# A two-block mixer on one core: attention's value product with float32 probabilities, two key tiles at a time in the two halves of the array's columns

## The chip, the core and the metric

The kernel runs on one core of one Trainium2 chip. The metric is the device time of one execution in microseconds; the median of several runs counts. One execution is profiled, and its trace is what the rows further down come from.

## What is computed

The program is a first block of two layers, then a second block of three mixers and a mixture of experts. The change lies in the first block's attention alone. Each layer has 8 heads; queries and keys have 96 features, values 64. In the first layer the 1024 tokens of `x` attend to all 1280 tokens (256 of the context and 1024 of `x`), and the 256 context tokens to themselves; in the second layer only the tokens of `x` have queries.

```python
def attend(q, k, v):
    ...
    def one_block(qi):
        s = jnp.einsum('bqhd,bkhd->bhqk', qi, k).astype(jnp.float32) * sm_scale
        p = jax.nn.softmax(s, axis=-1).astype(v.dtype)
        return jnp.einsum('bhqk,bkhd->bqhd', p, v)
```

Everything is float32, so products need more than the tensor engine's single pass over rounded operands.

## The kernel before, in words

**Products.** The kernel's usual form of an exact product is `mm3` (L100): each operand is two parts of type float32r, a high part rounded as the tensor engine does and the remainder, and three products (high by high, high by low, low by high) are summed in one PSUM bank; they are recorded under L104, L105 and L106. A product whose operands are plain float32 is one call in the text too, and two passes, each a weight load and a MATMUL, in the trace.

**Attention** (`attention`, L742) treats heads in pairs. `prepare` (L800) makes queries, keys and values of a pair by tokens, `turn` (L867) puts features on partitions in two parts by transposes (L876), `maxima` (L881) finds every query's largest score by products into the two banks `s1` (L891) and reductions on VectorE (L892), and puts it as one more row beside the queries (L900). `attend` (L905) does the rest, with keys on partitions: for a chunk of up to 512 queries and each tile of 128 keys, scores (L922), the exponential on ScalarE (L926), the probabilities in two parts (`ph`, a copy on ScalarE at L930 or in each chunk's second tile on VectorE at L928; `pl`, a subtraction at L931, every third one on GpSimd), and, three tiles later (`LAG`), three products with the values into one bank:

```python
v1, vl = vv[:, jv, hd, 64:], vv[:, jv, hd, :64]
nc.tensor.matmul(po[:65, :n], v1, ph, start=jv == 0, stop=False)
nc.tensor.matmul(po[:64, :n], vl, ph, start=False, stop=False)
nc.tensor.matmul(po[:65, :n], v1, pl, start=False, stop=jv == nk - 1)
```

These are L937, L938 and L939. The values `vv` hold a low part, a high part (L835 and L836) and a column of ones, so that row 64 of the result is the sum of the probabilities. At the end of a chunk ScalarE copies the bank (L942), the sums are put on the queries' partitions by one-row transposes (L946), inverted (L948), spread along the queries again by products with the identity (L952), multiplied into the gate (L954) and, on GpSimd, into the result (L955), which GpSimd's queue writes to DRAM (L956).

**Order.** Chunks are 256, 512 and 512 queries in the first layer (2, 10 and 10 key tiles) and 512 and 512 in the second. The loop at L967 takes the heads one after another; after every step of `attend` it advances the generators of the next pair's `prepare` and the next head's `turn` and `maxima` by set rates (`RP`, `RM`). That is the order of the text. The instructions on an engine are then placed by the library when the program is built, by when it expects their operands to be ready, earlier ones in the text first; once built, each engine's order is fixed. PSUM's 8 banks are three for scores (`st`), two for maxima (`s1`), and one each for the value product (`po`), for turns and sums (`tr`) and for `prepare` (`pre`). `up` holds the probabilities in `UB` buffers.

Of the kernel before, what the change touches and what calls it, by code (L numbers as in the profile page):

```python
# [20 lines left out]
P = 128  # L21
D = 1024
# [17 lines left out]
class K:  # L40
    """Engines, pools and constants that all phases share."""
# [23 lines left out]
    def psum(self, **bufs):  # L65
        """Banks by what they are for."""
        if self._ps:
            self._ps.close()
        self._ps = ExitStack()
        self.bufs = bufs or dict(mm=5, tr=2, po=1)  # L70
        self.ps = self._ps.enter_context(self.tc.tile_pool(name="ps", bufs=1, space=PSUM, reuse_waits="tile"))
# [7 lines left out]
    def rsqrt(self, out, in_, scale, eps):  # L79
        """out = (in_ * scale + eps) ** -0.5"""  # L80
# [8 lines left out]
    def split(self, hi, lo, src, scale=None, eng=None):  # L89
        """hi + lo = src (* scale, one number per partition), hi rounded as the tensor engine does."""  # L90
# [9 lines left out]
    def mm3(self, out, a, b, start, stop):  # L100
        """out += a^T b with both operands in two parts."""
# [6 lines left out]
    def mm_packed(self, both, top, a2, ah, bh, bl, start, stop):  # L108
        """both += a2^T bh and top += ah^T bl; a2 has the two parts of a side by side, top is both's first half,
        and the sum of both's halves is a^T b."""  # L110
# [8 lines left out]
    def vectors(self, pool, name, rows):  # L119
        """Vectors from DRAM (each a multiple of P long) as columns [P, n]: {key: column range}."""  # L120
# [16 lines left out]
    def bcast_row(self, out, col):  # L137
        """out[:, j] = col[j] for every partition: a column of P numbers as a row on all partitions."""
# [5 lines left out]
def vec(ap):  # L144
    """A DRAM vector (n * P,) as rows [n, P]."""
    return ap.rearrange("(n p) -> n p", p=P)


def gemv(k, pool, out, cs, w, b, ncols, chunk=128, group=4, tag="mm", ttag="tr", bufs=4):
    """out[:, j, :] = w[:, j * P:(j + 1) * P]^T cs + b[:, j], cs [P, KD, 2]; in steps."""  # L150
# [22 lines left out]
def run(gen, n=None):  # L173
    """The next n steps of a generator, or all that are left."""
# [19 lines left out]
HID = 99  # L194
PLP = 3
LAG = 3
UB = 6
# [23 lines left out]
def beside(main, side, n):  # L221
    """Steps of main, with n of side after every one."""
# [16 lines left out]
def put_h(k, wp, xn, tok, hh, hl, g, sh, onv=2):  # L239
    """(xn * g + sh) for a token tile, transposed and in two parts; onv of four features' tiles on the vector  # L240
    engine."""
# [20 lines left out]
def load_w(k, pool, w, c0, n, kt=KD, scale=None, tag="w", wmax=P, ktmax=KD, bufs=2, rbufs=2, rpool=None):  # L262
    """Columns c0..c0+n of w [kt * P, :] in two parts, [P, kt, n]."""
# [12 lines left out]
def head_weights(k, pool, I, l, pr, v, own=None):  # L276
    """Weights of a pair of heads' queries, and of its keys and values, in two parts, scaled by the norms'; in the
    places of the input product's weights, the parts in the pool own if there is one."""
# [15 lines left out]
class Columns:  # L294
    """Weights' tiles of P columns one after another, in turns in two pools; the first may be loaded ahead."""
# [12 lines left out]
def product(k, w, h, t0, n):  # L308
    """A bank with w^T h over n tokens from t0 on."""
# [7 lines left out]
def silu_out(k, sg, ps, dst):  # L317
    """silu(ps) into DRAM by way of sg."""
# [16 lines left out]
def block1(k, I, x_open, x_out, ahead, fill):  # L335
    """The first block: both layers; x_open(pool), then x_out(pool, t, tile) for the x token tiles, and
    what x_open returns, each of which returns what is to be done later; ahead: the next
    block's first weights, then a product with them; fill(pool): steps to be done beside the second layer's attention."""
    nc, tc = k.nc, k.tc
    A = nc.vector  # L340
    with ExitStack() as es:
# [16 lines left out]
        def early(pool=None):  # L358
            """The second layer's first weights, then a product with them."""
# [7 lines left out]
        def vectors(l):  # L367
            """The layer's vectors and tables."""
# [21 lines left out]
        def modulation(l, gp, **kw):  # L390
            """Shift and scale, then the gate."""
# [11 lines left out]
        def second(gp, **kw):  # L403
            """What the second layer needs."""
# [13 lines left out]
        def begin(wp):  # L418
            """The first layer's input."""
# [25 lines left out]
        for l in range(2):  # L445
# [26 lines left out]
            def weights():  # L472
                """In the place of what only the preparations need: the output's weights."""
# [15 lines left out]
def in_proj(k, I, l, last, h, vecs, keep, wp, ydram, sga_d, begin):  # L489
    """The layer's input product and its two convolution branches; begin(pool) makes the input."""  # L490
# [5 lines left out]
    with ExitStack() as es:  # L496
# [6 lines left out]
        def each(c0, n, cks, fn):  # L503
            """fn(feature tile, chunk of tokens, PSUM) over columns c0..c0+n of the input's product."""
# [2405 lines left out]
```

## Time and profile before

| | us |
|---|---|
| median of 3 runs | 4433.74 |
| lowest and highest | 4425.26, 4436.02 |
| span of the profiled execution | 4414.7 |
| TensorE (PE) busy, 22375 products | 4045.3 |
| VectorE (DVE) busy | 2878.1 |
| ScalarE (ACT) busy | 1983.2 |
| GpSimd (POOL) busy | 1231.9 |

The span runs from the first to the last instruction of the profiled execution, whose whole time is not listed apart; it is set beside the median of the runs. PE stands for products, PEld for the weight loads that overlap them. A product's recorded time is longer than the distance to the next one, because products are pipelined: what it costs is read from the starts.

### The profile page before, as it was taken

To read this page: it belongs to the slowest core of one execution; us is meant where nothing else is said; L and a number is where in the kernel's file an instruction comes from. 1 tells how busy PE (TensorE), PEld (TensorE's weight loads), DVE (VectorE), ACT (ScalarE), POOL (GpSimd) and SP (SyncE) were. 2 spreads that over 40 slices of the span, in tenths; PEclk is the share of its full clock that TensorE was granted. 3 is DMA by queue.
4 is the path that set the end of the run, shared out by engine and by line. 5 is a ranking of instruction groups with operands and counts; after the bars stand their busy time and mean duration, and the time that the engine had idled before them with its cause. 6 is when DMAs were issued, how large, how long until landed. Compare 5 with 4: busy or idle time off the path is not lost. (4 is left out here: it accounts for less than half of the span.)

```text
span 4414.7 us, 61941 instructions
## 1 busy us (share of the span) xinstructions
PE 4045.3 (92%) x22375; PEld 3077.3 (70%) x22376; DVE 2878.1 (65%) x5659; ACT 1983.2 (45%) x4292; POOL 1231.9 (28%) x1211
## 2 busy tenths in 40 slices
PE   7999899999998999999997999999898898899993
PEld 5787666667776666788785788777776566666672
DVE  4684577764745778646764555667776676776775
ACT  4122366653112766423443133433256566666664
POOL 1201133332101333321334331122313333343233
PEclk9999999999999999999997999899999999999996
DMA  6121400123123001334434411215368888888885
GB/s 187 34 64 43 123 13 13 33 83 107 41 61 102 11 10 36 121 117 129 126 118 136 122 34 33 74 44 189 110 228 264 242 265 247 256 276 264 269 274 165
DMA packets 371316, 558.81 MB, mean 127 GB/s; under 512 B 52126, under 2 KB 285056, under 8 KB 346048
## 3 DMA queue, kind: packets, MB, share of 16 engines
q1 hardware_dynamic: 335728, 432.81, 30.5%
q0 software_dynamic: 35280, 122.02, 10.7%
q8 instruction: 177, 2.90, 0.3%
q14 instruction: 131, 1.07, 0.1%
HBM read 438.42 MB, written 116.33 MB: 126 GB/s over the span
## 5 line engine op out<-in xcount | busy, mean ns | idle before, releaser
L95 DVE TENSOR_TENSOR wa_lo<-w_raw,wa_hi 128x512 fp32r<-128x512 f32 x520 | 338.1, 685 | 18.6 <-ACT wa_hi L94 17.8
L94 ACT ACTIVATE wa_hi<-w_raw 128x512 fp32r<-128x512 f32 x520 | 299.7, 626 | 59.9 <-PE mm L106 24.9
L104 PE MATMUL mm<-hh,w_hi 128*128 128x512 f32 (+1 forms) x848 | 320.0, 377 | 4.7 <-ACT h L256 4.7
L105 PE MATMUL mm<-hl,w_hi 128*128 128x512 f32 (+1 forms) x848 | 318.7, 376 | 0.0
L106 PE MATMUL mm<-hh,w_lo 128*128 128x512 f32 (+1 forms) x848 | 317.1, 374 | 0.0
L104 PE MATMUL mm<-wa_hi,xh 128*128 128x512 f32 (+3 forms) x632 | 268.0, 424 | 2.8 <-ACT xh L94 2.7
L106 PE MATMUL mm<-wa_hi,xl 128*128 128x512 f32 (+3 forms) x632 | 259.4, 410 | 3.6 <-DVE xl L95 3.6
L105 PE MATMUL mm<-wa_lo,xh 128*128 128x512 f32 (+3 forms) x632 | 261.3, 414 | 1.2 <-DVE wa_lo L95 1.2
L892 DVE TENSOR_REDUCE mx<-mm 128x1 f32<-128x512 f32 (+1 forms) x400 | 225.1, 587 | 53.2 <-PE mm L891 50.7
L926 ACT ACTIVATE pe<-mm 128x512 f32<-128x512 f32 (+1 forms) x336 | 193.2, 588 | 144.3 <-PE mm L106 115.5
L931 POOL TENSOR_TENSOR pl<-pe,ph 128x512 fp32r<-128x512 f32 x96 | 142.0, 1482 | 335.4 <-ACT ph L930 326.5
L931 DVE TENSOR_TENSOR pl<-pe,ph 128x512 fp32r<-128x512 f32 (+1 forms) x240 | 204.6, 864 | 38.1 <-ACT ph L930 36.8
L2698 POOL COPY wc<-xg 128x1 f32<-128x1 f32 (+5 forms) x97 | 79.6, 820 | 508.4 <-DMA xg<-h_d,ix 502.3
L2635 POOL DMA_INDIRECT acc_d<-ye,ix x97 | 168.7, 1740 | 182.5 <-ACT hidh L94 73.4
L159 PE MATMUL mm<-gemv_w,b_c_cs 128*2 128x128 f32 x1536 | 199.0, 286 | 10.2 <-DMA gemv_w<-in_w_mod_dram 7.1
L2631 ACT ACTIVATE ye<-mm,wc 128x512 f32<-128x512 f32 (+5 forms) x194 | 127.6, 680 | 176.7 <-DMA acc_d<-ye,ix 125.1
L595 DVE SCALAR_TENSOR_TENSOR acc<-zc,b_v,acc 128x512 f32<-128x512 f32 (+1 forms) x300 | 199.3, 713 | 1.5
L104 PEld LDWEIGHTS mm<-hh,w_hi 128*128 128x128 f32 x848 | 161.3, 190 | 40.1 <-issue 7.6
L105 PEld LDWEIGHTS mm<-hl,w_hi 128*128 128x128 f32 x848 | 161.4, 190 | 33.8 <-issue 7.0
L94 ACT ACTIVATE w_hi<-w_raw 128x1024 fp32r<-128x1024 f32 x61 | 64.6, 1059 | 262.5 <-PE mm L105 227.2
L106 PEld LDWEIGHTS mm<-hh,w_lo 128*128 128x128 f32 x848 | 161.2, 190 | 28.1 <-issue 0.4
L930 ACT ACTIVATE ph<-pe 128x512 fp32r<-128x512 f32 (+1 forms) x296 | 178.0, 625 | 4.1
(779 smaller groups left out, 11572.8 us busy)
## 6 DMA issues: line engine op xcount, KB each, us to landing
w_raw<-in_exp_w_dram SPq DMA_DIRECT2D x192, 1024.0 KB
w_raw<-in_w_in_dram SPq DMA_DIRECT2D x69, 512.0 KB
gemv_w<-in_w_mod_dram SPq DMA_DIRECT2D x48, 512.0 KB
gemv_w<-in_ada_w_dram SPq DMA_DIRECT2D x48, 512.0 KB
rec<-rec SPq DMA_DIRECT2D x64, 256.0 KB
wo_raw<-in_w_out_dram SPq DMA_DIRECT2D x20, 512.0 KB
y<-ydram SPq DMA_DIRECT2D x36, 256.0 KB
xt<-in_x_dram SPq DMA_DIRECT2D x16, 512.0 KB
```

The source lines that it names most:

```text
L94: nc.scalar.activation(hi, src, AF.Copy)
L95: eng.tensor_tensor(lo, src, f32(hi), op=OP.subtract)
L104: mm(out, ah, bh, start=start, stop=False)
L105: mm(out, ah, bl, start=False, stop=False)
L106: mm(out, al, bh, start=False, stop=stop)
L159: nc.tensor.matmul(ps[:2, c0:c0 + chunk], cs[:, kk], wt[:, kk], start=kk == 0, stop=kk == KD - 1)
L595: nc.vector.scalar_tensor_tensor(o, zc[:, ft, p0 + j:p0 + j + c[1]], v["cfw"][:, 2 * j + ft:2 * j + ft + 1], o, op0=OP.mult, op1=OP.add)
L892: nc.vector.tensor_reduce(mx[:, t, c:c + 1], ps[:, :n], axis=AX.X, op=OP.max)
L926: nc.scalar.activation(pe, ps, AF.Exp)
L930: nc.scalar.activation(ph, pe, AF.Copy)
L931: (nc.gpsimd if j % PLP == PLP - 1 else nc.vector).tensor_tensor(pl, pe, f32(ph), op=OP.subtract)
L2635: nc.gpsimd.indirect_dma_start(out=self.acc_d, out_offset=bass.IndirectOffsetOnAxis(ap=st.ix[:n, 0:1], axis=0), in_=y[:n], in_offset=None, ...
```

## The change

The values stay plain float32, 64 columns a head, without a low part and ones. The exponential's result is used as it is: the copies and subtractions at L928 to L931 go. Value products are issued for two key tiles together, with plain float32 operands, the first tile's into rows 0 to 63 of the bank and the second's into rows 64 to 127, that is, in the two halves of the array's columns. The sums of the probabilities come from additions of whole tiles, even tiles on GpSimd and odd ones on VectorE, in two running sums that VectorE merges at the end of a chunk; a product of each 128 x 128 part of the merged sum with a column of ones takes the place of the transposes. ScalarE copies the bank's lower rows and VectorE adds the upper ones to them. `UB` goes from 6 to 8. All else in the diff takes out comments, and is left out here.

```diff
-HID = 99
-PLP = 3
...
-UB = 6
+UB = 8
...
-        vals = [p.tile([P, NT, 2, 129], R32, name=f"vv{i}") for i, p in enumerate((kp, pp))]
+        vals = [p.tile([P, NT, 2, 64], F32, name=f"vv{i}") for i, p in enumerate((kp, pp))]
...
-            nc.scalar.activation(vals[i].rearrange("p t h n -> p (t h) n")[:, :, 128:],
-                                 k.ones[:, :2 * NT].unsqueeze(2), AF.Copy)
...
-                    rv = r2[:, t + e, 1:2]
-                    vh = vv[:, t + e, :, 64:128]
-                    nc.scalar.activation(vh, kv4[:, e, :, 64:], AF.Copy, scale=rv)
-                    nc.vector.scalar_tensor_tensor(vv[:, t + e, :, :64], kv4[:, e, :, 64:], rv, f32(vh), op0=OP.mult,
-                                                   op1=OP.subtract)
+                    nc.scalar.activation(vv[:, t + e], kv4[:, e, :, 64:], AF.Copy, scale=r2[:, t + e, 1:2])
...
-                parts = {}
+                pes, acc = {}, [None, None]
                 for j in range(nk + LAG):
                     if j < nk:
...
-                        pe = up.tile([P, 512], F32, name="pe")[:, :n]
-                        ph = up.tile([P, 512], R32, name="ph")[:, :n]
-                        pl = up.tile([P, 512], R32, name="pl")[:, :n]
+                        pe = pes[j] = up.tile([P, 512], F32, name="pe")[:, :n]
                         nc.scalar.activation(pe, ps, AF.Exp)
-                        if j % HID == 1:
-                            nc.vector.tensor_copy(ph, pe)
-                        else:
-                            nc.scalar.activation(ph, pe, AF.Copy)
-                        (nc.gpsimd if j % PLP == PLP - 1 else nc.vector).tensor_tensor(pl, pe, f32(ph), op=OP.subtract)
-                        parts[j] = ph, pl
-                    if j >= LAG:
-                        jv = j - LAG
-                        ph, pl = parts.pop(jv)
-                        v1, vl = vv[:, jv, hd, 64:], vv[:, jv, hd, :64]
-                        nc.tensor.matmul(po[:65, :n], v1, ph, start=jv == 0, stop=False)
-                        nc.tensor.matmul(po[:64, :n], vl, ph, start=False, stop=False)
-                        nc.tensor.matmul(po[:65, :n], v1, pl, start=False, stop=jv == nk - 1)
+                        e = j % 2
+                        if j == 2 + e:
+                            acc[e] = up.tile([P, 512], F32, name=f"acc{e}", bufs=2)[:, :n]
+                        if j >= 2:
+                            (nc.vector if e else nc.gpsimd).tensor_tensor(acc[e], pes[e] if j == 2 + e else acc[e], pe,
+                                                                          op=OP.add)
+                    if j >= LAG and (j - LAG) % 2:
+                        for e in range(2):
+                            jv = j - LAG - 1 + e
+                            nc.tensor.matmul(po[64 * e:64 * e + 64, :n], vv[:, jv, hd], pes[jv], start=jv < 2,
+                                             stop=jv >= nk - 2)
                     yield
-                y = sp.tile([65, 512], F32, name="y")[:, :n]
-                nc.scalar.activation(y, po[:65, :n], AF.Copy)
+                if nk == 2:
+                    acc = [up.tile([P, 512], F32, name="acc1", bufs=2)[:, :n]] * 2
+                    nc.vector.tensor_tensor(acc[1], pes[0], pes[1], op=OP.add)
+                else:
+                    nc.vector.tensor_tensor(acc[1], acc[1], acc[0], op=OP.add)
+                y = sp.tile([64, 512], F32, name="y")[:, :n]
+                nc.scalar.activation(y, po[64:, :n], AF.Copy)
                 ps = k.bank(tag="tr")
                 for j in range(n // P):
-                    nc.tensor.transpose(ps[:, j:j + 1], y[64:65, j * P:j * P + P], k.ident[64:65, 64:65])
+                    nc.tensor.matmul(ps[:, j:j + 1], acc[1][:, j * P:j * P + P], k.ones[:, :1], start=True, stop=True)
                 rc = sp.tile([P, 4], F32, name="rc")[:, :n // P]
                 nc.vector.reciprocal(rc, ps[:, :n // P])
+                nc.vector.tensor_tensor(y, po[:64, :n], y, op=OP.add)
                 yield
...
-                nc.gpsimd.tensor_tensor(y[:64], y[:64], sga, op=OP.mult)
-                nc.gpsimd.dma_start(ydram[row:row + 64, s], y[:64])
+                nc.gpsimd.tensor_tensor(y, y, sga, op=OP.mult)
+                nc.gpsimd.dma_start(ydram[row:row + 64, s], y)
```

## Rows read from the trace of the kernel before

**Rows 1.** The page's head: span, and the engines' busy time and share.

```profile
span 4414.7 us, 61941 instructions
...
PE 4045.3 (92%) x22375; PEld 3077.3 (70%) x22376; DVE 2878.1 (65%) x5659; ACT 1983.2 (45%) x4292; POOL 1231.9 (28%) x1211
```

**Rows 2.** By stretch: busy PE, PEld, DVE, ACT, POOL (count); granted clock, DMA share, GB/s.

```profile
532.00:945.00 413.00, 389.63 (x1994) 265.65 (x1993) 321.81 (x607) 266.28 (x692) 134.76 (x107) 0.99 0.09 25
1440.00:1804.00 364.00, 349.62 (x1756) 238.03 (x1755) 286.91 (x536) 249.34 (x619) 127.94 (x87) 1.00 0.09 24
```

**Rows 3.** Timeline of TensorE's products: start and length in us, line, shapes, count.

```profile
640.28 0.39 PE L938 MATMUL mm<-ph,vv 128*64 128x512 f32 x1
640.52 0.40 PE L939 MATMUL mm<-pl,vv 128*65 128x512 f32 x1
```

**Rows 4.** The page's costliest groups: parts of the probabilities (busy, mean ns | idle before).

```profile
L931 DVE TENSOR_TENSOR pl<-pe,ph 128x512 fp32r<-128x512 f32 (+1 forms) x240 | 204.6, 864 | 38.1 <-ACT ph L930 36.8
...
L930 ACT ACTIVATE ph<-pe 128x512 fp32r<-128x512 f32 (+1 forms) x296 | 178.0, 625 | 4.1
```

**Rows 5.** By line: L937's products; who waited for L931 (us, times).

```profile
L937 PE MATMUL mm<-ph,vv x336: 274/396/755, 532.2 to 1804.3; 128*65 128x512 f32 x160, 128*65 128x256 f32 x8
...
  PEld mm L939: 27.2, 35
...
  PE mm L939: 13.8, 17
```

**Rows 6.** TensorE's timeline around L522, float32 with 512 columns.

```profile
97.94 1.02 PE L522 MATMUL sm<-sq,ones 128*2 128x512 f32 x2
98.89 0.50 PE L105 MATMUL mm<-hl,w_hi 128*128 128x512 f32 x1
```

**Rows 7.** TensorE's timeline: float32 passes of 128 columns, two halves and one.

```profile
2500.36 0.44 PE L1732 MATMUL mm<-M,U 128*64 128x128 f32 x4
...
602.40 0.65 PE L952 MATMUL mm<-ident,rc 128*64 128x128 f32 x4 [0.53 <-DVE kl L98]
```

**Rows 8.** TensorE's timeline around two groups of L952, each of eight passes.

```profile
1490.09 0.39 PE L106 MATMUL mm<-qh,kl 97*128 97x512 f32 x1
1490.41 1.09 PE L952 MATMUL mm<-ident,rc 128*64 128x128 f32 x8
...
1491.71 0.40 PE L938 MATMUL mm<-ph,vv 128*64 128x512 f32 x1
...
932.22 0.40 PE L106 MATMUL mm<-qh,kl 97*128 97x512 f32 x1
...
933.90 0.40 PE L105 MATMUL mm<-ql,kh 97*128 97x512 f32 x1
```

**Rows 9.** TensorE's timeline: sums as transposes; L1479's passes, and its durations by line.

```profile
699.97 0.39 PE L104 MATMUL mm<-qh,kh 97*128 97x512 f32 x1
700.29 0.40 PE L946 MATMUL mm<-ident,y 1*128 1x1 f32 x4
...
700.96 0.39 PE L106 MATMUL mm<-qh,kl 97*128 97x512 f32 x1
...
2035.79 0.50 PE L1479 MATMUL mm<-c_hones,k 128*128 128x2 f32 x4
...
L1479 PE MATMUL mm<-c_hones,k x40: 165/251/251, 1998.3 to 2255.9; 128*128 128x2 f32 x40
```

**Rows 10.** TensorE's timeline: the first and last L937 of 53 not followed by L938.

```profile
548.22 0.39 PE L937 MATMUL mm<-ph,vv 128*65 128x512 f32 x1
548.46 0.38 PE L876 MATMUL mm<-ident,q 128*96 128x128 f32 x2
...
1775.03 0.39 PE L937 MATMUL mm<-ph,vv 128*65 128x512 f32 x1
1775.35 0.40 PE L946 MATMUL mm<-ident,y 1*128 1x1 f32 x4
```

**Rows 11.** By line: VectorE's low parts of the values.

```profile
L836 DVE SCALAR_TENSOR_TENSOR vv<-mm,r,vv x80: 330/351/355, 444.2 to 1675.6; 128x128 fp32r<-128x128 f32 x80
```

## The prediction

> **What bounds the kernel now.** I went from the whole to the stage. The page gives TensorE busy 92% of a span of 4414.7 us [rows 1], but that is a mean over stages, and the chain that ended last covers only the last tables of the kernel, so it says nothing of attention. The table by stretches does: value products run in two stretches, 532 to 945 us (first layer) and 1440 to 1804 us (second), 777 us together, where TensorE is busy 739, VectorE 609, ScalarE 516, GpSimd 263, at a granted clock of 0.99 and 1.00, its 2.4 GHz level [rows 2]. So TensorE bounds both, and a stall on it costs its full length. A busy TensorE says little of pace, so I read that from starts: products of 512 columns with float32r operands follow each other every 0.23 us although each is recorded with 0.40, and L938, which uses 64 columns of the array, keeps that pace between neighbours that use 65 [rows 3]; for 256 columns I take half. Beside them stand the copies and subtractions that make the two parts: 296 copies on ScalarE, 240 of the 336 subtractions on VectorE and so 96 on GpSimd [rows 4]. They matter only where L939 waits for them.
>
> **The value product.** Each line has 336 products [rows 5], one per key tile: 8 heads times 2+10+10 tiles in the first layer, 10+10 in the second; 16 of the 336 have 256 columns. Removed: 320 x 3 x 0.23 + 16 x 3 x 0.115 = 226 us of TensorE.
> Added: 160 pairs of 512 columns and 8 of 256. The nearest product with plain float32 and 512 columns is L522: two passes, and from its start to the next line 0.95 us [rows 6]; 0.09 of that is the change of array form found below, so 0.86. That two halves run side by side is shown by L1732, two float32 products into rows 0 to 63 and 64 to 127: its four passes last 0.44 us, while four of L952, all in one half, last 0.65 and eight 1.09, thus 0.11 a pass [rows 7, 8]. Two passes of L952 would last 0.43, so L1732's second half is free. A pair therefore costs 0.86: 160 x 0.86 + 8 x 0.43 = 141 us. The other bound, two halves in turn, doubles this; I take the first, because L1732 has the same form.
> **The change of form.** Going to a 64-column float32 tile and back costs time. Around L952 at 1490 us, from L106 to the second product behind it is 1.62 us, of which 2 x 0.23 and 8 x 0.11 are work: 0.28 lost. At 932 us the same sum gives 0.34 [rows 8]. I take 0.30 for each of 168 pairs, 50 us (bounds 47 and 57), since pairs stand among score products.
> **The sums.** Four transposes of one row cost now 0.53 with their change of form (L104 to L106 at 700 us, 0.99, less 2 x 0.23), with two transposes about 0.40: 32 x 0.53 + 8 x 0.40 = 20 us. The new ones load 128 x 128 float32 sums twice each, which L1479 does at 0.11 a pass (four in 0.50, the shortest 0.165): 288 x 0.11 = 32 [rows 9]. Net +12.
> **Stalls that go.** L939 waited for the subtractions: 13.8 us as seen by the product, 27.2 as seen by its weight load, overlapping [rows 5]. Bounds 14 and 27; I take 20. What comes late next is the other side work, whose waits stay.
> **Other engines.** ScalarE loses 296 copies (178 us), VectorE 240 subtractions (205 us), the other 40 copies and 80 of L836 (28 us), and gets 168 adds and merges and 40 sums of the halves, at L931's mean of 0.86 180 us; GpSimd gets 128 adds for 96 subtractions [rows 4, 11]. No cost is taken for any of these, because TensorE covers them; were it VectorE that bounds, it would still have 53 us less than its 609. No DMA is added or moved: L956 stays behind L955 on GpSimd, a few adds later, and only the output product reads what it writes. Of L836, twenty lie before the stretches: bounds 0 and 7 us, I take 2.
> **The new wait.** At a chunk's end the sums need the merge on VectorE, which waits for GpSimd's last add; behind the waiting merge stand VectorE's maxima, for which TensorE waits. Bounds: one merge of 0.86 for each of 40 chunks, 34 us, against a gain of 18: in the stretches TensorE is idle for 777 - 739 = 38 us [rows 2], 20 of them are counted already, and VectorE's and ScalarE's queues get shorter. They are taken as equal, 0.
> **Pairs that are torn.** This is what the diff does not show. Instructions stand on TensorE in the order in which the build expected them to be ready, not that of the text. L937 and L938 have their operands at the same time, yet in 53 of 336 cases another line stands between them: first at 548 us, last at 1775 [rows 10]. Between two products of the old form that cost nothing. Between two halves of a pair it makes each run alone: 0.86 and one more excursion of 0.30, 1.16 us. At the same share, 16%, 27 pairs x 1.16 = +31 us. Lower bound 0. Upper: a foreign product enters when it becomes ready during the first half, and that is 0.86/0.23 = 3.7 times as long as L937; 1 - 0.84^3.7 gives 48%, 81 pairs, +94 us. I take the row's own share: the half lasts longer, but VectorE, which makes side work late, is less loaded afterwards.
>
> **The sum.** -226 + 141 + 50 + 12 - 20 - 2 + 0 + 31 = -14 us. The profiled execution is given by its span, 4414.7; the runs have a median of 4433.74, 19 us more, which lie around the span and which the change doesn't touch. So 4433.7 - 14 gives 4420 us. A measurement of this kernel can tell about 0.3%, 13 us, from no change.
>
> A page states an order that speaks against this change. The row comes first: L1732's four passes fill two pass times, not three. By the Trainium skill ("TensorE: Matmul & The Clock Gate", section on the mechanism of packing) matmuls start and end strictly in program order; then the first half's second pass would hold back the second half's first, a pair would take three pass times, and the sum would be 71 us higher. The trace disagrees by 0.11 us in that one row.
>
> **Rivals.**
> *Pairs stay whole.* Nothing comes between the halves, as in the row of L1732. For: 283 of 336 neighbours stay together even now. Against: the first half lasts much longer than L937. Then the sum is -45: 4389.
> *Pairs are torn in four of ten to a half.* Place: between the two value products; price 1.16 us each. From 39 torn pairs on (45/1.16), 23%, the gain is gone. At 45%, 76 pairs: -45 + 88 = +43, 4477. For: the maxima's products have two PSUM banks and enter wherever VectorE frees one. Against: half as many borders between value products, and less work on VectorE.
> *The halves don't run together.* Then 168 pairs cost a second time, 141 us, and torn pairs only lose the excursion: -45 + 141 + 8 = +104, 4538. L1732 speaks against it, though with 128 columns.
> *Passes keep program order.* Three pass times, 0.43 more for 160 pairs and 0.21 for 8: 4420 + 71 = 4491.
> *The attention gives nothing.* What is saved on TensorE is waited for at the merge and at the maxima (34 us there, the rest by the adds of VectorE and GpSimd): 4434.
>
> **How the numbers follow.** Forecast 0.44 (4400 to 4440 by its unknown terms), whole pairs 0.20, torn 0.23, halves apart 0.04, program order 0.04, nothing gained 0.05. Of the forecast half lies below 4420, the rest within 13 us but for a tenth. Faster: 0.22 + 0.20 + 0.02 of the torn = 0.44. Same: 0.17 + 0.05 + 0.04 of the torn = 0.26. Slower: 0.05 + 0.17 + 0.08 = 0.30. The low end is whole pairs with stalls of 27 and L836 at 7: -45 - 12 = -57, 4376. The high end reaches to most torn pairs: 4472. Outside are the two packing failures (0.08), some torn ones (0.08) and little below.
>
> **What would show it.** Value products in twos of two passes, the second starting within some ns of the first, about 0.86 to the next line plus 0.3 at its borders; no L939 wait; the sums at 0.9 us a chunk; the two stretches some 7 us shorter each. Wrong: more than 23% of the pairs with a foreign line between their halves, passes of the halves in turn, or TensorE waiting 0.5 us or more for most merges.

## The result, and the profile after

The changed kernel takes 4458.61 us (median of 4 runs, 4452.56 to 4462.22); the kernel before, run beside it, 4434.16 (4 runs, 4425.26 to 4436.02). The ratio is 1.0066 with a 95% interval of 1.0045 to 1.0086: **slower by 24.5 us**, where 14 us faster was forecast. Its time lies in the range.

The line numbers are those of the changed kernel: scores L104 to L106, exponential L916, adds of probabilities L921, value products L926, merge L933, sums L939, spreading L946, maxima L882 and L883. First the page's head, which answers to [rows 1].

```profile
span 4460.5 us, 61187 instructions
...
PE 4100.5 (92%) x22184; PEld 3014.9 (68%) x22184; DVE 2806.8 (63%) x5507; ACT 1822.7 (41%) x3992; POOL 1308.6 (29%) x1243
```

It says as little as before: TensorE at 92%, and all other engines but GpSimd with less work. The two stretches with value products say more. This is the view of [rows 2] for the changed kernel: window, its length, busy PE, PEld, DVE, ACT and POOL (count), granted clock, DMA share, GB/s.

```profile
531.00:968.00 437.00, 429.90 (x1896) 239.37 (x1894) 282.91 (x537) 188.76 (x541) 164.19 (x123) 0.95 0.09 25
1459.00:1835.00 376.00, 370.17 (x1646) 202.89 (x1644) 259.33 (x473) 167.66 (x466) 145.09 (x103) 1.00 0.08 25
sum 813.00, PE 800.08 PEld 442.26 DVE 542.24 ACT 356.43 POOL 309.28; mean PE 400.04 PEld 221.13 DVE 271.12 ACT 178.22 POOL 154.64
```

The stretches grew from 777 to 813 us. VectorE, ScalarE and the weight loads have less to do, as intended, and TensorE is idle for 813 - 800 = 13 us in place of 38; but it is busy 61 us longer. So the loss lies in TensorE's busy time and not in its waits. Part of it is the clock, 0.95 in place of 0.99 in the first layer; the greater part is work. TensorE's timeline shows what work (start and length in us, line, shapes, passes):

```profile
573.68 1.08 PE L926 MATMUL mm<-pe,vv 128*64 128x512 f32 x4
574.69 0.50 PE L104 MATMUL mm<-qh,kh 97*128 97x512 f32 x1
...
537.40 1.07 PE L926 MATMUL mm<-pe,vv 128*64 128x512 f32 x2
538.40 0.36 PE L104 MATMUL mm<-w_hi,cqh 128*128 128x192 f32 x1
...
539.82 0.38 PE L867 MATMUL mm<-ident,k__3442 128*96 128x128 f32 x2
540.13 1.07 PE L926 MATMUL mm<-pe,vv 128*64 128x512 f32 x2
541.13 0.50 PE L104 MATMUL mm<-qh,kh 97*128 97x512 f32 x1
```

At 573.68 stands a whole pair: four passes, 1.01 us to the next line. At 537.40 and 540.13 stand two halves alone, with twelve products of `prepare` and two turns (L867) between them: two passes each, and 1.00 us each. A lone half costs as much as a pair. Two counts are used from here on. A *half time* is the 0.86 us that a half takes, alone or with another half beside it. An *excursion* is one run of value products between other products, with the change of form at both its ends. In the order of the built program 101 of the 168 pairs have a foreign product between their halves (103 in the trace, by the starts); since halves of different pairs sometimes meet, the value products fill 249 half times in 223 excursions, where whole pairs would fill 168 half times.

The new wait cost nothing. By line, this is L933, the merge, with what waited for it (us, times):

```profile
L933 DVE TENSOR_TENSOR acc<-acc,acc x32: 665/682/910, 557.6 to 1835.0; 128x512 f32<-128x512 f32 x32
...
  PE mm L939: 0.9, 2
```

And the sums cost what [rows 9] gave, 0.11 a pass: eight in 0.92 us to the next line (timeline):

```profile
636.22 1.05 PE L939 MATMUL mm<-ones,acc 128*128 128x1 f32 x8
637.14 0.34 PE L106 MATMUL mm<-w_hi,cql 128*128 128x192 f32 x1
```

### The profile page after: what moved, and what is told of

Its sections match the earlier page's. It is cut to its first block, busy times and chain, and to the rows that moved or that the text cites. A ratio compares the mean times of both kernels' runs of the same rounds, so it can differ in the third digit from the quotient of the medians.

```text
span 4460.5 us, 61187 instructions
## 1 busy us (share of the span) xinstructions
PE 4100.5 (92%) x22184; PEld 3014.9 (68%) x22184; DVE 2806.8 (63%) x5507; ACT 1822.7 (41%) x3992; POOL 1308.6 (29%) x1243
## 5 line engine op out<-in xcount | busy, mean ns | idle before, releaser
L104 PE MATMUL mm<-hh,w_hi 128*128 128x512 f32 (+1 forms) x848 | 318.0, 375 | 3.5 <-ACT h L254 3.5
L106 PE MATMUL mm<-hh,w_lo 128*128 128x512 f32 (+1 forms) x848 | 315.3, 372 | 0.0
L883 DVE TENSOR_REDUCE mx<-mm 128x1 f32<-128x512 f32 (+1 forms) x400 | 225.7, 589 | 110.0 <-PE mm L882 107.5
L916 ACT ACTIVATE pe<-mm 128x512 f32<-128x512 f32 (+1 forms) x336 | 193.7, 589 | 229.8 <-PE mm L106 203.4
L104 PE MATMUL mm<-wa_hi,xh 128*128 128x512 f32 (+3 forms) x632 | 269.8, 427 | 8.1 <-ACT xh L94 8.1
L926 PE MATMUL mm<-pe,vv 128*64 128x512 f32 (+1 forms) x672 | 265.3, 620 | 0.0
L106 PE MATMUL mm<-wa_hi,xl 128*128 128x512 f32 (+3 forms) x632 | 260.7, 412 | 2.7 <-DVE xl L95 2.7
L2692 POOL COPY wc<-xg 128x1 f32<-128x1 f32 (+5 forms) x97 | 92.7, 956 | 500.6 <-DMA xg<-h_d,ix 495.5
L104 PEld LDWEIGHTS mm<-hh,w_hi 128*128 128x128 f32 x848 | 160.1, 189 | 38.5 <-issue 7.6
L921 POOL TENSOR_TENSOR acc<-acc,pe 128x512 f32<-128x512 f32 x96 | 140.5, 1464 | 141.8 <-ACT pe L916 140.5
L104 PE MATMUL mm<-wb_hi,hidh 128*128 128x512 f32 (+5 forms) x420 | 178.3, 425 | 1.7 <-ACT hidh L94 1.7
L106 PEld LDWEIGHTS mm<-hh,w_lo 128*128 128x128 f32 x848 | 160.0, 189 | 27.5 <-issue 0.4
L159 PEld LDWEIGHTS mm<-gemv_w,b_c_cs 128*2 128x2 f32 x1536 | 127.0, 88 | 70.0 <-issue 8.5
```

Of the source, the lines that this page charges most:

```text
L104: mm(out, ah, bh, start=start, stop=False)
L106: mm(out, al, bh, start=False, stop=stop)
L159: nc.tensor.matmul(ps[:2, c0:c0 + chunk], cs[:, kk], wt[:, kk], start=kk == 0, stop=kk == KD - 1)
L883: nc.vector.tensor_reduce(mx[:, t, c:c + 1], ps[:, :n], axis=AX.X, op=OP.max)
L916: nc.scalar.activation(pe, ps, AF.Exp)
L921: (nc.vector if e else nc.gpsimd).tensor_tensor(acc[e], pes[e] if j == 2 + e else acc[e], pe, op=OP.add)
```

## The experiments

**How the runs are compared.** Times are given as ratios to the kernel before on the same chip, whose medians were 4416 to 4426 us there. To see inside a ratio, I split the stretches' length (from the first value product to the last, both layers) into three: idle (length less busy PE); the time at TensorE's lower level, 1.2 GHz, from the granted clock in stretches of 2 us ((1 - clock) x 2 x length); and TensorE's **own work**, busy less half of the time at the lower level. The last is my estimate from the first two, good to some us. Each split is of one execution, which can lie some way off the median of its runs (20 us for alone, 4512.17 against 4491.7, and up to 15 for the others).

| kernel | ratio (95%) | stretches | idle | at 1.2 GHz | own work | half times, excursions |
|---|---|---|---|---|---|---|
| before | 1 | 777 | 38 | 14 | 732 | |
| changed | 1.0066 (1.0045 to 1.0086) | 813 | 13 | 42 | 779 | 249, 223 |
| whole | 0.9917 (0.9894 to 0.9939) | 740 | 28 | 35 | 695 | 168, 152 |
| alone | 1.0157 (1.0125 to 1.0190) | 851 | 21 | 37 | 811 | 275, 253 |
| oneside | 1.0252 (1.0223 to 1.0281) | 883 | 34 | 48 | 826 | 336, 164 |
| noadd | 0.9925 (0.9900 to 0.9950) | 746 | 27 | 62 | 688 | 168, 161 |
| swap | 0.9941 (0.9920 to 0.9962) | 745 | 27 | 19 | 708 | 179, 161 |
| quad | 1.0064 (1.0041 to 1.0088) | 810 | 53 | 161 | 676 | 168, 100 |
| whole_spread | 1.0120 (1.0096 to 1.0143) | 827 | 81 | 177 | 658 | 168, 140 |
| quad_spread | 1.0157 (1.0129 to 1.0185) | 837 | 108 | 182 | 639 | 168, 95 |
| prioswap | 1.0070 (1.0043 to 1.0097) | 807 | 42 | 136 | 696 | 168, 127 |
| quad_s13 | 0.9949 (0.9932 to 0.9966) | 756 | 49 | 63 | 676 | 168, 100 |
| whole_s13 | 0.9902 (0.9876 to 0.9928) | 731 | 22 | 32 | 693 | 168, 156 |
| whole_ub10 | 0.9943 (0.9921 to 0.9965) | 754 | 24 | 72 | 694 | 168, 149 |
| after_s13 | 1.0040 (1.0028 to 1.0051) | 807 | 23 | 32 | 768 | 243, 220 |
| swap_s13 | 0.9894 (0.9874 to 0.9915) | 739 | 22 | 36 | 699 | 172, 160 |

**whole: the halves kept together.** The later tile's product comes first in the text, and the other is tied behind it.

```diff
-                        for e in range(2):
-                            jv = j - LAG - 1 + e
-                            nc.tensor.matmul(po[64 * e:64 * e + 64, :n], vv[:, jv, hd], pes[jv], start=jv < 2,
-                                             stop=jv >= nk - 2)
+                        def half(jv, e):
+                            return nc.tensor.matmul(po[64 * e:64 * e + 64, :n], vv[:, jv, hd], pes[jv], start=jv < 2,
+                                                    stop=jv >= nk - 2)
+                        jv = j - LAG - 1
+                        with tc.issue_after(half(jv + 1, 1).ins), tc.high_priority():
+                            half(jv, 0)
```

> The changed kernel with the two halves of a pair kept next to each other on TensorE's queue. In the changed kernel's order 101 of 168 pairs have another product between their halves; the value products fill 249 half times (0.86 us each) in 223 excursions; here no pair is torn: 168 half times, 152 excursions. Theory torn pairs: 81 x 0.86 + 71 x 0.30 = 91 us less than the changed kernel, 4368 us (4350 to 4385), faster than the kernel before by 1 to 2%. Rival, the sums (adds on VectorE and GpSimd, the merge) or the exponentials set the pace and a torn pair only fills time that is waited for anyway: within 15 us of the changed kernel, 4445 to 4465, with TensorE idle in the stretches instead of busy.

Measured: 4380.2 us, 0.9917 of the kernel before, 1.5% under the changed kernel. The time lies in the expected range; the gain on the kernel before, 0.8%, falls short of the 1 to 2% expected. The view by stretches:

```profile
531.00:932.00 401.00, 382.14 (x1895) 228.01 (x1894) 288.85 (x536) 189.06 (x541) 165.99 (x123) 0.96 0.10 28
1427.00:1766.00 339.00, 329.94 (x1641) 194.38 (x1639) 261.47 (x473) 166.80 (x465) 143.40 (x103) 1.00 0.09 26
sum 740.00, PE 712.08 PEld 422.38 DVE 550.32 ACT 355.86 POOL 309.39; mean PE 356.04 PEld 211.19 DVE 275.16 ACT 177.93 POOL 154.69
```

TensorE is busy 88 us less than in the changed kernel with nearly the same products; its own work is 84 us less, against 91 expected. 15 us of that come back as idle time: part of the torn time had covered stalls. The rival, by which torn pairs only filled waiting time, falls.

**alone: a bigger dose of tearing.**

```diff
-                    if j >= LAG and (j - LAG) % 2:
-                        for e in range(2):
-                            jv = j - LAG - 1 + e
-                            nc.tensor.matmul(po[64 * e:64 * e + 64, :n], vv[:, jv, hd], pes[jv], start=jv < 2,
-                                             stop=jv >= nk - 2)
+                    if j >= LAG:
+                        jv = j - LAG
+                        e = jv % 2
+                        nc.tensor.matmul(po[64 * e:64 * e + 64, :n], vv[:, jv, hd], pes[jv], start=jv < 2,
+                                         stop=jv >= nk - 2)
```

> A bigger dose: the changed kernel with one half product at every step, not two at every second one. In its order the value products fill 275 half times in 253 excursions, against 249 and 223 in the changed kernel. Theory torn pairs: 26 x 0.86 + 30 x 0.30 = 31 us slower than the changed kernel, 4490 us (4475 to 4505). Rival, the sums set the pace: no slower than the changed kernel, 4445 to 4465.

Measured: 1.0157; 0.9% or 40 us more than the changed kernel. Its own work is 811 - 779 = 32 us more, where 31 were expected. The price goes with the dose.

**oneside: both halves in the same columns.** The edit is against whole. ScalarE and VectorE now both read rows 0 to 63; in the change itself ScalarE copies rows 64 to 127 and VectorE adds rows 0 to 63 to the copy.

```diff
-                            return nc.tensor.matmul(po[64 * e:64 * e + 64, :n], vv[:, jv, hd], pes[jv], start=jv < 2,
-                                                    stop=jv >= nk - 2)
+                            return nc.tensor.matmul(po[:64, :n], vv[:, jv, hd], pes[jv], start=jv == 1,
+                                                    stop=jv == nk - 2)
...
-                nc.scalar.activation(y, po[64:, :n], AF.Copy)
+                nc.scalar.activation(y, po[:64, :n], AF.Copy)
...
-                nc.vector.tensor_tensor(y, po[:64, :n], y, op=OP.add)
+                nc.vector.tensor_tensor(y, po[:64, :n], y, op=OP.max)
```

> The kernel with whole pairs, but both products of a pair go to rows 0 to 63 of the bank, the same columns of the array, one after the other; 164 excursions. It takes away the running side by side and nothing else. Theory that two halves in different columns run at once and cost 0.86 together: 160 x 0.86 + 8 x 0.43 = 141, and 12 x 0.30 = 4, so 145 us slower than the kernel with whole pairs, 4513 if that is at 4368. Rival, passes keep program order (three pass times a pair): 70 us slower only. Rival, the halves never ran at once: the same time as the kernel with whole pairs.

Measured: 1.0252, 3.4% or 148 us over whole pairs; the own work is 131 us more. The timeline of one pair:

```profile
572.95 1.93 PE L925 MATMUL mm<-pe,vv 128*64 128x512 f32 x4
574.81 0.38 PE L891 MATMUL mm<-nident,mx 128*1 128x128 f32 x2
```

The same four passes take 1.86 us to the next line, where a pair in two halves took 1.01: 0.85 us, the 0.86 of the prediction. The rivals (three pass times; no running side by side) fall. By the Trainium skill ("TensorE: Matmul & The Clock Gate", section on the mechanism of packing) matmuls start and end strictly in program order; three pass times for a pair would follow, and the pair's 1.01 us does not agree, as L1732 had not [rows 7].

**noadd: without the sums.** Against whole: the eight adds of a chunk and the merge are left out; the reciprocal is taken of one tile's probabilities, raised to at least one.

```diff
-                        if j >= 2:
-                            (nc.vector if e else nc.gpsimd).tensor_tensor(acc[e], pes[e] if j == 2 + e else acc[e], pe,
-                                                                          op=OP.add)
...
-                    nc.vector.tensor_tensor(acc[1], acc[1], acc[0], op=OP.add)
+                acc = up.tile([P, 512], F32, name="acc1", bufs=2)[:, :n]
+                nc.vector.tensor_tensor(acc, pes[nk - 1], k.ones[:, :1].to_broadcast([P, n]), op=OP.max)
```

> The kernel with whole pairs without the sums: the running sums and the merge are left out, and the reciprocals are taken of one tile's probabilities, raised to at least one by one operation on VectorE; so GpSimd and VectorE lose 128 adds each and no wait for GpSimd is left at a chunk's end. 161 excursions. Theory that the merge and the adds are covered by TensorE: within 15 us of the kernel with whole pairs. Rival, TensorE waits one merge of 0.86 us a chunk or more for them: 34 us faster or more.

Measured: 0.9925, the same as whole pairs. By stretches:

```profile
sum 746.00, PE 719.21 PEld 428.01 DVE 434.36 ACT 357.69 POOL 116.82; mean PE 359.61 PEld 214.01 DVE 217.18 ACT 178.85 POOL 58.41
```

VectorE has 116 us and GpSimd 193 us less to do, and TensorE's idle time stays where it was, 27 us against 28: adds and merge are covered.

**swap: why pairs are torn.** One exchange in the changed kernel, with nothing that ties the halves.

```diff
-                        for e in range(2):
+                        for e in (1, 0):
```

> The changed kernel with one thing exchanged: of the two value products the later tile's stands first in the text; nothing holds them together. If a pair was torn because its second operand came ready one exponential after its first, pairs now stay together nearly all: the order has 11 torn pairs (101 before) and 161 excursions. Then 11 x 0.86 + 9 x 0.30 = 12 us above the kernel with whole pairs, a ratio to the kernel before of 0.994 (0.991 to 0.998). Rival, what tore them is any product that becomes ready while the first half runs, which the exchange doesn't touch: as the changed kernel, 1.005 or more.

Measured: 0.9941, the number expected. So the order of the two products in the text is what tears the pairs; the rival falls. Why it does is my reading and was not tested by itself: the first tile's operand is one exponential older; with its product first in the text, that is placed as soon as the build expects it to be ready, and the second when its own exponential is expected, so what comes ready between stands between. With the later tile first, both are ready when the first is placed. Nothing waits for this on the chip: if exponentials and value products are matched in their order in the changed kernel's trace, the second tile's exponential had ended before the first half started in all but one of the torn pairs, by 5 us in the median. The order was fixed when the program was built.

**quad: four tiles at a time.** `half` is the function of whole; its start and stop flags move to the first and last product of each half of the bank.

```diff
-UB = 8
+UB = 10
...
-                    if j >= LAG and (j - LAG) % 2:
...
+                    m = j - LAG + 1
+                    if m > 0 and (m % 4 == 0 or m == nk):
+                        g = range(m - 1, (m - 1) // 4 * 4 - 1, -1)
+                        with tc.issue_after(half(g[0], 1).ins), tc.high_priority():
+                            for jv in g[1:]:
+                                half(jv, jv % 2)
```

> Whole pairs, and two pairs together: four key tiles at a time (4, 4 and 2 of a chunk's ten), 100 excursions in place of 152, ten buffers for probabilities in place of eight. Theory that an excursion costs 0.30: 52 x 0.30 = 16 us less than whole pairs, ratio 0.988. Rival, an excursion costs only the 0.06 longer way in that the rows of whole pairs show (0.29 against 0.23 from the line before): 3 us, ratio 0.991. Rival, waiting for four exponentials leaves TensorE idle: slower than whole pairs.

Measured: 1.0064, 65 us slower than whole pairs, although the own work is 19 us less, as 52 excursions of 0.30 should give. Idle time and clock took more than that. The view by stretches of 2 us around one stall (columns as above):

```profile
688.00:690.00 2.00, 2.00 (x11) 1.45 (x9) 0.72 (x1) 0.60 (x1) 2.00 (x2) 1.00 0.00 0
690.00:692.00 2.00, 0.12 (x1) 0.00 (x0) 0.00 (x0) 0.00 (x0) 2.00 (x1) 1.00 0.00 0
692.00:694.00 2.00, 0.20 (x1) 0.20 (x2) 1.83 (x5) 0.49 (x5) 0.13 (x1) 0.85 0.00 0
694.00:696.00 2.00, 2.00 (x6) 1.05 (x6) 1.77 (x7) 1.68 (x9) 0.11 (x1) 0.50 0.00 0
696.00:698.00 2.00, 2.00 (x7) 0.66 (x8) 0.50 (x2) 0.36 (x1) 2.00 (x2) 0.50 0.01 4
698.00:700.00 2.00, 2.00 (x7) 0.39 (x4) 0.00 (x0) 0.00 (x0) 2.00 (x1) 0.50 0.00 0
700.00:702.00 2.00, 2.00 (x8) 0.50 (x8) 0.91 (x3) 0.00 (x0) 1.05 (x1) 0.94 0.00 0
```

TensorE does almost nothing for 3.7 us, and then its granted clock is 0.50, its 1.2 GHz level, for some 7 us of full work: the stall costs twice. The timeline across it names the cause:

```profile
688.00 4.14 POOL L87 TENSOR_TENSOR fq<-fq,mhalf 128x20 f32<-128x20 f32 x1
...
692.17 0.18 DVE L843 SCALAR_TENSOR_TENSOR fq<-fq,r 128x20 f32<-128x20 f32 x1 [3.45 <-POOL fq L87]
...
693.33 1.01 DVE L883 TENSOR_REDUCE mx<-mm 128x1 f32<-128x256 f32 x2
...
693.80 0.80 PE L882 MATMUL mm<-kh,qh 96*128 96x512 f32 x1 [3.68 <-DVE mx L883]
```

VectorE waits for a power that GpSimd computes for `prepare`, the maxima's reductions stand behind it on VectorE, and TensorE waits for a bank of theirs. The waits of VectorE for these powers (us, times, longest), here:

```profile
DVE fkn L842 <- POOL fk L838: 21.1, 6, 4.6
...
DVE fq L843 <- POOL fq L87: 18.3, 6, 4.0
```

and with whole pairs:

```profile
DVE fkn L842 <- POOL fk L838: 10.2, 3, 3.4
...
DVE fq L843 <- POOL fq L87: 7.5, 4, 3.8
```

39 us against 18. The two waits are the same as with whole pairs, but they are more, 12 against 7. Why four tiles at a time make them so was not tested.

**whole_spread and quad_spread: the sums by one product.**

```diff
-                for j in range(n // P):
-                    nc.tensor.matmul(ps[:, j:j + 1], acc[1][:, j * P:j * P + P], k.ones[:, :1], start=True, stop=True)
-                rc = sp.tile([P, 4], F32, name="rc")[:, :n // P]
-                nc.vector.reciprocal(rc, ps[:, :n // P])
...
-                    nc.tensor.matmul(ps[:64, j * P:(j + 1) * P], rc[:, j:j + 1].to_broadcast([P, 64]), k.ident,
-                                     start=True, stop=True)
-                nc.vector.tensor_tensor(sga, ps[:64, :n], sga, op=OP.mult)
+                nc.tensor.matmul(ps[:64, :n], k.ones[:, :64], acc[1], start=True, stop=True)
...
+                rc = sp.tile([64, 512], F32, name="rc")[:, :n]
+                nc.vector.reciprocal(rc, ps[:64, :n])
+                nc.gpsimd.tensor_tensor(sga, rc, sga, op=OP.mult)
```

> Whole pairs, and the sums put on 64 rows by one float32 product of a 128 x 64 block of ones with the merged sum, in place of the products with one column, the reciprocal of 128 x 4 and the spreading products with the identity; the reciprocal is then of 64 x 512 on VectorE, and the product with the gate goes to GpSimd. Per chunk of 512 queries TensorE loses 0.9 + 1.09 + one excursion of 0.3 and gets 0.86: 32 x 1.4 + 8 x 0.7 = 50 us less than whole pairs, ratio 0.980. Rival, the longer reciprocal holds up the maxima behind it on VectorE, for which TensorE waits: within 10 us of whole pairs, or slower.

> Both of the last two edits. If they add, 16 + 50 us less than whole pairs: ratio 0.977 to the kernel before, and faster than both kernels. Rival, with TensorE's own work gone the exponentials and reductions set the pace: no better than the better of the two alone.

Measured: 1.0120 and 1.0157. The rivals were right, and the two edits together are worse than either alone. The own work of whole_spread falls by 37 us, but by line the reciprocal of whole_spread is (minimum, median, maximum in ns)

```profile
L944 DVE RECIPROCAL rc<-mm x40: 1736/3345/3350, 536.0 to 1857.7; 64x512 f32<-64x512 f32 x32, 64x256 f32<-64x256 f32 x8
```

These are 3.35 us in which VectorE reduces no maxima. TensorE is idle for 81 us and spends 177 at its lower level; the largest of its waits by line, 22 us, is for the last reduction of VectorE's maxima (L885). That the reciprocal makes them is argued: it was not run without the other edits.

**quad_s13, whole_s13, whole_ub10, prioswap: which part of quad hurt.** quad_s13 is quad and whole_s13 is whole, each with three banks for the maxima and two for the scores; whole_ub10 is whole with ten buffers; prioswap is the changed kernel and puts both value products ahead of all that is ready.

```diff
-ATPS = dict(st=3, s1=2, po=1, tr=1, pre=1)
+ATPS = dict(st=2, s1=3, po=1, tr=1, pre=1)
```

> Four tiles at a time, with three PSUM banks for the maxima and two for the scores, in place of two and three. If four tiles at a time lost time because TensorE comes back after 1.9 us to maxima whose two banks VectorE has not freed, the waits for L883 (20 us with four tiles) fall under 5 us, the clock's falls with them, and the time falls by 20 us or more: ratio under 1.002. Rival, the stalls come from VectorE's own order (every wait for it grew, not that one alone): no change, or more waits for the exponentials with two banks for scores: 1.005 or more.

> The control: whole pairs with three banks for the maxima and two for the scores. By the theory of the banks it gains little, since its waits for L883 are 5 us: ratio 0.990 to 0.994. If two banks for scores cost by themselves, over 0.996.

```diff
-UB = 8
+UB = 10
```

> The other control: whole pairs with ten buffers for probabilities, as four tiles at a time had. If the buffers alone changed the order for the worse, over 1.000; if it was the grouping, within 0.3% of whole pairs, 0.989 to 0.995.

```diff
-                        for e in range(2):
+                        with tc.high_priority():
+                          for e in (1, 0):
```

> The later tile first, and both value products ahead of everything else that is ready, without a tie between them: no torn pair, 127 excursions against 152 of the kernel with whole pairs. Theory (an excursion costs between 0.06 and 0.30, stalls unchanged): 2 to 8 us less than whole pairs, ratio 0.990 to 0.9915. Rival, value products bunched in front (up to ten in a row) make the maxima and scores late, TensorE stalls and its clock falls as with four tiles at a time: slower than whole pairs.

Measured: 0.9949, 0.9902, 0.9943 and 1.0070. The third bank gives four tiles at a time 1.1%, 50 us, back, and 98 us of the time at the lower level. But the sign named for the theory did not come: the waits of L882 for L883 stay at 17 us in the two stretches (20 with two banks), in 7 waits in place of 19, and idle time falls by 4 us only. Nearly all of the gain is clock, 98 / 2 = 49 us. Why nearly the same idle time costs so much less clock with the third bank stays open. The stretches of quad_s13,

```profile
sum 756.00, PE 707.41 PEld 433.29 DVE 560.02 ACT 354.79 POOL 304.91; mean PE 353.70 PEld 216.65 DVE 280.01 ACT 177.39 POOL 152.46
```

and of whole_s13,

```profile
sum 731.00, PE 708.82 PEld 428.86 DVE 557.74 ACT 357.95 POOL 301.75; mean PE 354.41 PEld 214.43 DVE 278.87 ACT 178.97 POOL 150.87
```

give the price of an excursion: 156 - 100 = 56 fewer, 693 - 676 = 17 us less own work, 0.30 each. The figure is rough, as own work is: prioswap has 25 excursions fewer than whole and 696 us of own work against 695. The starts around one excursion give a little more (timeline of whole):

```profile
573.23 0.39 PE L106 MATMUL mm<-qh,kl 97*128 97x512 f32 x1
573.45 0.63 PE L882 MATMUL mm<-kh,qh 96*128 96x512 f32 x2
574.01 1.08 PE L925 MATMUL mm<-pe,vv 128*64 128x512 f32 x4
575.02 0.50 PE L104 MATMUL mm<-qh,kh 97*128 97x512 f32 x1
575.36 0.28 PE L882 MATMUL mm<-kh,qh 96*128 96x256 f32 x1
```

From 573.23 to 575.36 are 2.13 us, of which 4 x 0.23 and 0.86 are work: 0.35 lost. By the Trainium skill ("TensorEngine Tiling (Array Packing)", section Key Properties) a change of the tiling mode drains the engine; that a change of form costs time agrees with these runs, and a drain as such they don't show. L938, with 64 columns but float32r operands, pays nothing [rows 3], so the columns alone don't make the price; whether the float32 operands do was not tried. Four tiles at a time still lose to pairs, because 49 us are idle and 63 at the lower level, against 22 and 32. Ten buffers cost little or nothing by themselves: 0.9943 lies within the expected bounds, and overlaps the interval of whole pairs. Bunching value products in front is bad: 136 us at the lower level, the rival of that run.

**after_s13 and swap_s13: banks or order.** The bank edit alone in the changed kernel, and with the exchange of swap.

```diff
-ATPS = dict(st=3, s1=2, po=1, tr=1, pre=1)
+ATPS = dict(st=2, s1=3, po=1, tr=1, pre=1)
...
-                        for e in range(2):
+                        for e in (1, 0):
```

> The changed kernel with three PSUM banks for the maxima and two for the scores, its halves as torn as before: 92 pairs, 243 half times, 220 excursions (249 and 223 in the changed kernel). If torn halves make the loss, the banks don't mend it: 6 x 0.86 + 3 x 0.30 = 6 us and some stalls less than the changed kernel, ratio 1.003 to 1.007. Rival, what was lost is TensorE's stalls on the maxima and the clock that falls behind them (the changed kernel had 42 us at the lower level, the kernel before 14): with the third bank that goes, and the ratio is under 1.000.

> The changed kernel with the later tile's product first in the text and three banks for the maxima: 4 torn pairs, 160 excursions, no tie and no priority. If order and banks add as they did with whole pairs: 0.990 to 0.993, faster than both kernels with two small edits. If the tie was needed, 0.996 or more.

Measured: 1.0040 and 0.9894. With the third bank the changed kernel spends 32 in place of 42 us at the lower level and is still slower than the kernel before; so the banks alone do not mend it. With the halves exchanged too it is 1.1% faster than the kernel before, by two short edits. The third bank helps the exchanged version (0.9894 against 0.9941, intervals apart); swap_s13, whole_s13 and whole are not told apart by their intervals.

## Why the prediction was wrong

**What held.** The rival with whole pairs was put at -45 us; measured with whole pairs -37 (0.9917, between -47 and -27). Single prices were measured too: a pair's second half free (oneside, 148 us for taking it away against 145), 0.30 to 0.35 an excursion (quad_s13 against whole_s13, and the starts in whole), 0.11 a pass of the sums, merge and adds covered (0.9 us of waiting; noadd). The 0.09 that the prediction takes off L522 for the change of form is worked out nowhere in it; the 0.86 holds all the same, since a pair and its two further pass times differ by 0.85 (oneside).

That the sum without torn pairs comes within 8 us is in part luck, because three misses nearly cancel. Own work was to fall by 226 - 141 - 50 - 12 = 23 us and fell by 37, some 5 of it because there are 152 excursions and not 168. Idle time was to fall by 22 and fell by 10, from 38 to 28: the waits of L939 are gone, but other waits took half their place. The changed kernel's 13 us of idle time are no proof of the term, since torn halves cover stalls. And the clock, which the sum does not have, took (35 - 14) / 2 = 10 us.

**What failed: "at the same share, 16%".** The share of torn pairs was taken from L937 and L938 [rows 10], whose operands come ready at the same time; the prediction says so itself. The two halves of a pair read two tiles, and those come ready one exponential apart. The scaled upper bound, 48%, rested on the same share and on the wrong picture of a product that slips in during the first half; in the built order it is 101 of 168, 60%. The kernel before had a nearer row: L938 and L939, whose operands `ph` and `pl` come ready one after the other, have a foreign line between them in 112 of 336 cases by their starts, 33%. One of them (timeline of TensorE, before):

```profile
548.59 0.47 PE L938 MATMUL mm<-ph,vv 128*64 128x512 f32 x1
548.90 0.25 PE L104 MATMUL mm<-w_hi,cqh 128*128 128x192 f32 x1
...
550.22 0.40 PE L939 MATMUL mm<-pl,vv 128*65 128x512 f32 x1
```

At that share 56 pairs x 1.16 = 65 us, and the sum is -45 + 65 = +20, slower; the share is still only about half of what was built. The reason given for staying at 16%, that VectorE has less work, shows no part in it: what tears is the text's order of the two products (swap).

**What was mis-sized beside it.** A torn pair was priced at 1.16 us. Measured it is 84 / 101 = 0.83, since a lone half sometimes stands beside one of another pair, which saves a half time or an excursion. 101 x 0.83 = 84 in place of 31 makes the step 53 us too low. That is why the result is nearest to the rival of torn pairs (from 23% on slower) and yet stays under its 4477.

**What was not in the sum.** The prediction says that a stall on TensorE costs its full length; it leaves out TensorE's clock. The changed kernel spends 42 us at the lower level, the kernel before 14, which costs (42 - 14) / 2 = 14 us more. By the split of the table the stretches' growth is 47 of own work, less 25 of idle time, plus 14 of clock: 36, as measured. After_s13 has 32 at the lower level and is still slower, so the clock is the smaller part.

**The base.** The 19 us said to lie around the span do not lie there: the changed kernel's profiled execution took 4462.22 us with a span of 4460.5, 1.7 more. With as much around it, the profiled execution of before took about 4416 us, a quicker one than its listed runs (4425.26 at the least). So the spans differ by 46 us, and the medians by 24.5. Of the 46, 15 lie behind the last value product (4460.5 - 1835 against 4414.7 - 1804), where nothing was changed; how much of the 36 in the stretches is the quick execution too is not known.

## What to carry to other kernels

Two instructions that pay only side by side have to be put side by side: let the one whose operand comes last stand first in the text, or tie them, and count the torn ones in the built order before pricing the pair. A share of neighbours read from an old trace may be carried over only to operands that come ready in the same way: together, or one after the other. Work taken off TensorE is worth its length only where no stall takes its place. Where the edit put a long instruction or a long group in the way (a reciprocal of 3.35 us, four tiles at a time), the stalls were paid twice, as idle time and as time at the lower clock.

## What had not been expected of the hardware

A stall of TensorE costs more than its length: after 3.7 us without work its clock stood at 0.50 for about 7 us; in quad, 25 us more idle time than whole pairs came with 126 us more at the lower level. The ratio is not fixed: in quad_s13, 21 us more came with 28.

Small products of another line run beside a lone half. TensorE's timeline in the changed kernel:

```profile
849.36 0.27 PE L946 MATMUL mm<-ident,rc 128*64 128x128 f32 x1
849.37 0.64 PE L926 MATMUL mm<-pe,vv 128*64 128x512 f32 x1
849.47 0.49 PE L946 MATMUL mm<-ident,rc 128*64 128x128 f32 x3
849.80 1.02 PE L926 MATMUL mm<-pe,vv 128*64 128x512 f32 x3
```

L946 writes rows 0 to 63; a value product starts 0.01 us behind its first pass, and three more passes of L946 start within the 0.43 us of that product's first pass. So two products need not be the halves of one pair to share the array. It was not measured what that is worth.

A reciprocal on VectorE of 512 columns took 3.35 us, 6.5 ns a column, where a sum of two tiles of as many columns takes 0.68 (L933).
